# RMSNorm and SiLU on one core: the first three loads spread over both hardware DMA queues

## The chip, the cores and the metric

The kernel runs on one core of a Trainium2 chip. A core has engines that run side by side, each with its own instruction stream: VectorE (DVE in the profile), ScalarE (ACT), TensorE (PE), GpSimd (POOL) and SyncE (SP). Sixteen DMA engines move data between the chip's main memory (HBM) and the on-chip memory of 128 partitions (SBUF). Here ScalarE issues the loads and SyncE the stores, each over a hardware queue of its own; an issued transfer is cut into packets that the sixteen DMA engines carry.

The metric is the device time of one launch in microseconds (us), the median of several runs. Beside it there is one profiled execution, with every instruction and every DMA packet in its trace.

## The reference

```python
def setup_inputs():
    batch, seq_len, hidden = 8, 1024, 2048
    return {
        "x": np.random.randn(batch, seq_len, hidden).astype(np.float32),
        "gamma": np.random.randn(hidden).astype(np.float32),
        "eps": np.float32(1e-5),
    }

def reference(x, gamma, eps):
    rms = np.sqrt(np.mean(x ** 2, axis=-1, keepdims=True) + eps)
    out = gamma * x / rms
    return (out * (1 / (1 + np.exp(-out)))).astype(np.float32)
```

So 8192 rows of 2048 float32 are read, each row is divided by its root mean square, multiplied by gamma and passed through SiLU, and 8192 rows are written: 67.1 MB in and 67.1 MB out.

## The kernel before

The rows are cut into 16 blocks of 512 rows. A block lies in one tile `xt` of 128 partitions; a partition holds `J = 4` consecutive rows of x, 32 KB that are contiguous in main memory. Six tiles (`BUFS`) rotate, so a load needs the tile that the store six blocks before has left. All arithmetic on a block is done in place, and the store goes out from the same tile.

A block passes through these steps:

- `load` (line 54): one transfer of 4 MB, issued from ScalarE's queue.
- `squares_scalar` (line 65) and `squares_vector` (line 73): the sums of squares of its four rows per partition, one or two rows on ScalarE, the others on VectorE. The squares themselves go to a tile in PSUM that nobody reads.
- `root` on ScalarE (line 82) and `invert` on VectorE (line 87): the reciprocal of the root mean square.
- `multiply` on VectorE (line 92): row times reciprocal times gamma, one instruction per row.
- `silu` on ScalarE (line 98): two instructions, of two rows each, and then `store` (line 102), one transfer of 4 MB, issued from SyncE's queue.

The order of the work is written out by hand under `tc.manual_schedule()`. On each engine the instructions run in that order, and a DMA that an engine issues stands in the same order: an issue from ScalarE comes only after the ScalarE instructions ahead of it have been handed over. Semaphores between engines and DMAs are put in by the framework. It has eight for DMAs that it gives out in turn, so an issue can also carry a wait on an earlier transfer that had the same one.

At the start the six loads are issued one after another from ScalarE's queue. Then come two small fills on VectorE, a first activation on ScalarE that loads a table, and gamma's transfer of 8 KB, issued from SyncE (line 111). TensorE spreads gamma over all 128 partitions by multiplying it with a row of ones (line 114), and VectorE copies the result to `g` (line 115). The first use of `g` is `multiply(0)`.

The loop over blocks has three forms. For the first three blocks (`SOON`) the order is multiply(b), squares of b+1 on ScalarE, silu(b) with its store, squares of b+1 on VectorE, root(b+1). For the others up to block 13 the squares and the root of b+1 come first and multiply(b) and silu(b) after them. Block 14 goes in the first order again. Load b+3 is issued in the middle of `squares_scalar(b+1)`, behind its first activation, for blocks 6 to 15; since that activation needs block b+1, at most two loads are under way from then on. The last block is finished by a multiplication with gamma on VectorE and SiLU with the reciprocal as its scale on ScalarE (lines 152 and 154), and one last store.

Of the kernel before, what the change touches and what calls it, by code (L numbers as in the profile page):

```python
# [1 line left out]

# [4 lines left out]

ACT = mybir.ActivationFunctionType
ALU = mybir.AluOpType


@with_exitstack
def kernel(
    ctx: ExitStack,
    tc: tile.TileContext,
    x: bass.AP,
    gamma: bass.AP,
    eps: bass.AP,
    out: bass.AP,
):  # L20

    nc = tc.nc
    P = nc.NUM_PARTITIONS
    f32 = mybir.dt.float32
    x2 = x.flatten_outer_dims()
    o2 = out.flatten_outer_dims()  # L30
    n, d = x2.shape
    J = 4
    BUFS = 6
    nblk = n // (P * J)
    xb = x2.rearrange("(b p j) d -> b p (j d)", p=P, j=J)
    ob = o2.rearrange("(b p j) d -> b p (j d)", p=P, j=J)

    singles = ctx.enter_context(tc.tile_pool(name="singles", bufs=1))
    pool = ctx.enter_context(tc.tile_pool(name="pool", bufs=BUFS))
    small = ctx.enter_context(tc.tile_pool(name="small", bufs=2))  # L40
    psum = ctx.enter_context(tc.tile_pool(name="psum", bufs=1, space=bass.MemoryType.PSUM))

    Q = 4
    w = d // Q
    g = singles.tile([P, d], f32)
    eps_t = singles.tile([P, 1], f32)
    ones = singles.tile([P, P], f32)
    junk_a = psum.tile([P, d], f32, name="junk_a")
    junk_v = psum.tile([P, d], f32, name="junk_v")
    blocks, sss, rmss, rstds = {}, {}, {}, {}  # L50

    def load(b):
        xt = pool.tile([P, J * d], f32, name="xt")
        nc.scalar.dma_start(out=xt, in_=xb[b])  # L54
        blocks[b] = xt

    def row(b, j):
        return blocks[b][:, j * d:(j + 1) * d]

    def squares_scalar(b, loads=()):  # L60


        sss[b] = small.tile([P, J], f32, name="ss")
        for j in range(share(b)):
            nc.scalar.activation(out=junk_a, in_=row(b, j), func=ACT.Square,  # L65
                                 accum_out=sss[b][:, j:j + 1])
            if j == 0:
                for s in loads:
                    load(s)

    def squares_vector(b):
        for j in range(share(b), J):
            nc.vector.tensor_tensor_reduce(  # L73
                out=junk_v, in0=row(b, j), in1=row(b, j), scale=1.0, scalar=0.0,
                op0=ALU.mult, op1=ALU.add, accum_out=sss[b][:, j:j + 1])

    def share(b):
        return 1 if 4 <= b <= 12 and b % 2 == 0 else 2

    def root(b):  # L80
        rms = small.tile([P, J], f32, name="rms")
        nc.scalar.activation(out=rms, in_=sss.pop(b), func=ACT.Sqrt, scale=1.0 / d, bias=eps_t)  # L82
        rmss[b] = rms

    def invert(b):
        rstd = small.tile([P, J], f32, name="rstd")
        nc.vector.reciprocal(out=rstd, in_=rmss.pop(b))  # L87
        rstds[b] = rstd

    def multiply(b):  # L90
        for j in range(J):
            nc.vector.scalar_tensor_tensor(out=row(b, j), in0=row(b, j), scalar=rstds[b][:, j:j + 1],  # L92
                                           in1=g, op0=ALU.mult, op1=ALU.mult)

    def silu(b):
        for h in range(0, J, 2):
            cols = slice(h * d, (h + 2) * d)
            nc.scalar.activation(out=blocks[b][:, cols], in_=blocks[b][:, cols], func=ACT.Silu)  # L98
        store(b)

    def store(b):
        nc.sync.dma_start(out=ob[b], in_=blocks[b])

    with tc.manual_schedule():

        for b in range(BUFS):
            load(b)
        nc.vector.memset(ones, 1.0)  # L108
        nc.vector.memset(eps_t, float(eps))
        nc.scalar.activation(out=junk_a[:, 0:1], in_=ones[:, 0:1], func=ACT.Square)  # L110
        nc.sync.dma_start(out=g[0:1, :], in_=bass.AP(tensor=gamma.tensor, offset=gamma.offset, ap=[[d, 1], [1, d]]))
        for c in range(Q):
            cols = slice(c * w, (c + 1) * w)
            nc.tensor.matmul(junk_v[:, cols], ones[0:1, :], g[0:1, cols], start=True, stop=True)  # L114
        nc.vector.tensor_copy(out=g, in_=junk_v)  # L115

        last = nblk - 1
        SOON = 3  # L120
        squares_scalar(0)
        squares_vector(0)
        root(0)
        invert(0)
        for b in range(last):
            loads = [b + 3] if BUFS <= b + 3 < nblk else []
            if b < SOON:
                multiply(b)
                squares_scalar(b + 1, loads)
                silu(b)  # L130
                squares_vector(b + 1)
                root(b + 1)
            elif b < last - 1:
                squares_scalar(b + 1, loads)
                squares_vector(b + 1)
                root(b + 1)
                multiply(b)
                silu(b)
            else:
                multiply(b)  # L140
                squares_scalar(b + 1)
                silu(b)
                squares_vector(b + 1)
                root(b + 1)
            if b + 1 < last:
                invert(b + 1)


        for j in range(J):
            if j == J // 2:  # L150
                invert(last)
            nc.vector.tensor_mul(out=row(last, j), in0=row(last, j), in1=g)  # L152
        for j in range(J):
            nc.scalar.activation(out=row(last, j), in_=row(last, j), func=ACT.Silu,  # L154
                                 scale=rstds[last][:, j:j + 1])
        store(last)


# [1 line left out]
_INS = ['x', 'gamma', 'eps']  # L160
_OUTS = [((8, 1024, 2048), 'float32')]

_NUMBERS = {'eps': 9.999999747378752e-06}


# [26 lines left out]
```

## Time and profile before

| What | us |
| --- | --- |
| Median of 3 runs (317.01 to 317.69) | 317.03 |
| Span of the profiled execution, first to last instruction | 315.03 |
| VectorE busy, 157 instructions | 235.3 |
| ScalarE busy, 136 instructions | 213.8 |
| TensorE busy, 8 instructions | 7.2 |
| ScalarE idle for VectorE in front of silu (line 98) | 27.0 |
| VectorE idle for loads in front of its squares (line 73) | 42.3 |
| ScalarE idle for loads in front of its squares (line 65) | 22.5 |
| A load, issue to landing, shortest / median / longest | 12.3 / 38.7 / 81.8 |
| A store, issue to landing, shortest / median / longest | 13.5 / 28.6 / 33.7 |

The page of a profile gives the busy time of each engine, its share in 40 equal slices of the span, the DMA queues with their packets and bytes, and the chain of work that ended last. Further views give every instruction in order of time, who waited for whom, and busy time in stretches that one chooses.

Two queues carry nearly everything: 67.11 MB over the queue of ScalarE's issues (q10) and 67.12 MB over that of SyncE's issues (q1), at a mean of 426 GB/s over the span. These are some of the issues in order of time (start, duration, engine's queue and line, what):

```profile
0.73 2.97 ACTq L54 DMA_DIRECT2D xt<-in_x_dram  x6
0.73 0.34 SPq L111 DMA_DIRECT2D g<-in_gamma_dram  x1
...
66.81 0.33 ACTq L54 DMA_DIRECT2D xt<-in_x_dram  x1
...
84.99 0.34 ACTq L54 DMA_DIRECT2D xt<-in_x_dram  x1
```

The first six loads and gamma are issued at once, at 0.73; load 6 follows at 66.81 and load 7 at 84.99. The stores begin at 35.27.

### The profile page before, as it was taken

The page shows a single profiled execution, that of the slowest core. Times are in us where ns is not written, and L with a number is a line of the kernel's source. Part 1 is how long each engine was busy: PE and PEld are TensorE (multiplying, and loading weights), DVE is VectorE, ACT ScalarE, POOL GpSimd, SP SyncE. Part 2 cuts the span into 40 slices and gives each one's busy share as a digit, 9 for nine tenths or more (in the row PEclk, how much of TensorE's full clock was granted, in tenths as well). Part 3 has the DMA queues.
Part 4 walks back from the last instruction along what each step waited for, and adds up shares of the span by engine and source line. Part 5 has one row for each costly group of instructions (what it writes and reads, how often), then busy time and mean ns, then how long its engine had stood idle before and what let it go on. Part 6 is the DMA issues. An engine that isn't in the chain of part 4 may idle for free.

```text
span 315.0 us, 437 instructions
## 1 busy us (share of the span) xinstructions
PE 7.2 (2%) x8; PEld 2.5 (1%) x8; DVE 235.3 (75%) x157; ACT 213.8 (68%) x136; POOL 0.2 (0%) x4
## 2 busy tenths in 40 slices
PE   6200000000000000000000000000000000000000
PEld 3000000000000000000000000000000000000000
DVE  0679597979995795957959489593996939999600
ACT  1349998972799258782687727877288768779910
POOL 0000000000000000000000000000000000000000
DMA  8999999999999999999999999999999999999996
GB/s 334 399 466 399 399 466 399 466 399 466 399 467 404 459 416 449 420 445 420 445 420 445 420 445 420 445 424 445 420 445 429 437 429 437 429 437 433 433 433 300
DMA packets 4612, 134.24 MB, mean 426 GB/s; under 512 B 513, under 2 KB 513, under 8 KB 513
## 3 DMA queue, kind: packets, MB, share of 16 engines
q10 hardware_dynamic: 2304, 67.11, 49.8%
q1 hardware_dynamic: 2306, 67.12, 49.4%
q14 instruction: 2, 0.02, 0.0%
HBM read 67.12 MB, written 67.11 MB: 426 GB/s over the span
## 4 chain that ended last, share of the span: by engine, by line
DMA 68%; DVE 14%; ACT 11%; issue 2%; ACTq 1%; DVEq 0%
DMA xt<-in_x_dram 68%; DVE xt L92 9%; DVE junk_v L73 5%; ACT xt L98 4%; ACT junk_a L65 3%; ACT xt L154 2%; ACT L82 1%; ACTq L187 1%; ACT L154 0%; ACT L98 0%; ACT rms L82 0%; DVE ss L73 0%; DVE rstd L87 0%; ACTq L54 0%; ACTq L82 0%
## 5 line engine op out<-in xcount | busy, mean ns | idle before, releaser
L92 DVE SCALAR_TENSOR_TENSOR xt<-xt,rstd,g 128x2048 f32<-128x2048 f32 x60 | 137.0, 2345 | 0.1
L98 ACT ACTIVATE xt<-xt 128x4096 f32<-128x4096 f32 x30 | 108.3, 3615 | 27.0 <-DVE xt L92 27.0
L73 DVE CUSTOM_DVE_ANT_0 junk_v<-xt 128x2048 f32<-128x2048 f32 x37 | 85.1, 2299 | 43.0 <-DMA xt<-in_x_dram 42.3
L65 ACT ACTIVATE junk_a<-xt 128x2048 f32<-128x2048 f32 x27 | 50.6, 1876 | 22.8 <-DMA xt<-in_x_dram 22.5
L82 ACT ACT_TABLE_LOAD x15 | 19.2, 1283 | 27.4 <-DVE ss L73 27.3
L98 ACT ACT_TABLE_LOAD x14 | 18.0, 1283 | 0.2
L87 DVE RECIPROCAL rstd<-rms 128x4 f32<-128x4 f32 x16 | 2.7, 171 | 8.4 <-ACT rms L82 8.4
L152 DVE TENSOR_TENSOR xt<-xt,g 128x2048 f32<-128x2048 f32 x4 | 8.9, 2279 | 0.0
L115 DVE COPY g<-junk_v 128x2048 f32<-128x2048 f32 x1 | 2.3, 2292 | 8.6 <-PE junk_v L114 8.6
L82 ACT ACTIVATE rms<-ss,eps_t 128x4 f32<-128x4 f32 x16 | 4.8, 297 | 5.7 <-DVE ss L73 5.5
L154 ACT ACTIVATE xt<-xt,rstd 128x2048 f32<-128x2048 f32 x4 | 7.7, 1990 | 0.0
L114 PE MATMUL junk_v<-g,ones 1*128 1x512 f32 x8 | 7.2, 1073 | 2.4 <-DMA g<-in_gamma_dram 2.4
L73 DVE DVE_READ_ACCUMULATOR2_ANT ss<- 128x1 f32 x37 | 5.2, 140 | 0.0
L65 ACT ACTIVATION_READ_ACCUMULATOR junk_a<-xt 128x1 f32 x27 | 5.0, 186 | 0.0
L110 ACT ACT_TABLE_LOAD x1 | 1.3, 1283 | 3.7 <-issue 3.7
L114 PEld LDWEIGHTS junk_v<-g,ones 1*128 1x128 f32 x8 | 2.5, 326 | 5.5 <-issue 5.5
L154 ACT ACT_TABLE_LOAD x1 | 1.3, 1283 | 0.0
L108 DVE MEMSET ones<- 128x128 f32 x1 | 0.2, 165 | 0.8 <-PEq L173 0.8
L110 ACT ACTIVATE junk_a<-ones 128x1 f32<-128x1 f32 x1 | 0.2, 174 | 0.0
L173 POOL MEMSET const-bfloat16-1.0<- 128x1 bf16 x1 | 0.1, 103 | 0.0
L173 POOL MEMSET const-uint8-127<- 128x1 uint8 x1 | 0.1, 103 | 0.0
L173 POOL MEMSET const-float32-0.0<- 128x1 f32 x1 | 0.1, 99 | 0.2 <-issue 0.2
(2 smaller groups left out, 0.2 us busy)
## 6 DMA issues: line engine op xcount, KB each, us to landing
xt<-in_x_dram ACTq DMA_DIRECT2D x16, 4096.0 KB, 38.7
out_dram<-xt SPq DMA_DIRECT2D x16, 4096.0 KB, 28.6
g<-in_gamma_dram SPq DMA_DIRECT2D x1, 8.0 KB
```

The costliest lines, as they stand in the source:

```text
L65: nc.scalar.activation(out=junk_a, in_=row(b, j), func=ACT.Square, accum_out=sss[b][:, j:j + 1])
L73: nc.vector.tensor_tensor_reduce(out=junk_v, in0=row(b, j), in1=row(b, j), scale=1.0, scalar=0.0, op0=ALU.mult, op1=ALU.add, accum_out=sss ...
L82: nc.scalar.activation(out=rms, in_=sss.pop(b), func=ACT.Sqrt, scale=1.0 / d, bias=eps_t)
L87: nc.vector.reciprocal(out=rstd, in_=rmss.pop(b))
L92: nc.vector.scalar_tensor_tensor(out=row(b, j), in0=row(b, j), scalar=rstds[b][:, j:j + 1], in1=g, op0=ALU.mult, op1=ALU.mult)
L98: nc.scalar.activation(out=blocks[b][:, cols], in_=blocks[b][:, cols], func=ACT.Silu)
L110: nc.scalar.activation(out=junk_a[:, 0:1], in_=ones[:, 0:1], func=ACT.Square)
L114: nc.tensor.matmul(junk_v[:, cols], ones[0:1, :], g[0:1, cols], start=True, stop=True)
L115: nc.vector.tensor_copy(out=g, in_=junk_v)
L152: nc.vector.tensor_mul(out=row(last, j), in0=row(last, j), in1=g)
L154: nc.scalar.activation(out=row(last, j), in_=row(last, j), func=ACT.Silu, scale=rstds[last][:, j:j + 1])
L187: with _tile.TileContext(nc) as tc:
```

## The change

The loads of blocks 0 and 1 are each cut into two transfers: columns 0 to 4095 of the tile (the first two rows of a partition) over ScalarE's queue, columns 4096 to 8191 over SyncE's. Block 2 is loaded whole over SyncE's queue, where it stands in front of the stores. Blocks 3 and later are loaded over ScalarE's queue as before. Gamma's transfer is issued first, in front of the loads, still over SyncE's queue. No arithmetic is changed, and the order of the instructions on VectorE, TensorE and GpSimd stays as it was.

```diff
     BUFS = 6
+    PAIRED = 2
...
     def load(b):
         xt = pool.tile([P, J * d], f32, name="xt")
-        nc.scalar.dma_start(out=xt, in_=xb[b])
+        if b < PAIRED:
+            half = J * d // 2
+            nc.scalar.dma_start(out=xt[:, :half], in_=xb[b][:, :half])
+            nc.sync.dma_start(out=xt[:, half:], in_=xb[b][:, half:])
+        elif b == PAIRED:
+            nc.sync.dma_start(out=xt, in_=xb[b])
+        else:
+            nc.scalar.dma_start(out=xt, in_=xb[b])
         blocks[b] = xt
...
     with tc.manual_schedule():
 
+        nc.sync.dma_start(out=g[0:1, :], in_=bass.AP(tensor=gamma.tensor, offset=gamma.offset, ap=[[d, 1], [1, d]]))
         for b in range(BUFS):
             load(b)
         nc.vector.memset(ones, 1.0)
         nc.vector.memset(eps_t, float(eps))
         nc.scalar.activation(out=junk_a[:, 0:1], in_=ones[:, 0:1], func=ACT.Square)
-        nc.sync.dma_start(out=g[0:1, :], in_=bass.AP(tensor=gamma.tensor, offset=gamma.offset, ap=[[d, 1], [1, d]]))
```

On SyncE's queue the order is now gamma, the second half of block 0, the second half of block 1, block 2, and then the sixteen stores; on ScalarE's it is the first half of block 0, the first half of block 1, and blocks 3, 4 and 5. The framework's semaphores are given out in the new order, and with that the issue of block 5 from ScalarE carries a wait on gamma's transfer, which it did not before.

## The prediction

> **What bounds the kernel now.** I read the busy slices of the page first, then the queue table, then busy time and DMA by stretch, then the chain of waits, and last the trace's records of single DMA packets. In the slices:
>
> ```profile
> DVE  0679597979995795957959489593996939999600
> ACT  1349998972799258782687727877288768779910
> DMA  8999999999999999999999999999999999999996
> ...
> q10 hardware_dynamic: 2304, 67.11, 49.8%
> q1 hardware_dynamic: 2306, 67.12, 49.4%
> ```
>
> VectorE and ScalarE have holes everywhere; the DMA row has none between its first and its last slice. The two queues (q10 carries ScalarE's loads, q1 SyncE's gamma and stores) take 99.2% of sixteen engines' span. By stretch:
>
> ```profile
> 4.00:36.00 32.00, 5.57 (x7) 1.66 (x5) 20.95 (x14) 19.93 (x16) 0.00 (x0) 1.00 0.99 429
> 42.00:276.00 234.00, 0.00 (x0) 0.00 (x0) 188.89 (x127) 164.94 (x102) 0.00 (x0) 1.00 1.00 433
> 280.00:312.00 32.00, 0.00 (x0) 0.00 (x0) 16.25 (x11) 20.59 (x13) 0.00 (x0) 1.00 1.01 434
> ```
>
> The last column is GB/s. Loads alone (first row), loads and stores together (second) and stores alone (third) all run at the same rate. So the DMA engines have one ceiling, whoever asks, and the two queues share it; I call it the line.
>
> The packet records say how the span is made. Each block is 128 rows of 32 KB, so each of 16 DMA engines carries 8 packets per block and 256 in all for 16 loads and 16 stores. A 32 KB record takes 1.213 us, and records follow each other every 1.210 us (blocks 1 and 2 end 9.68 us apart, 9.68 / 8). The first packets start at 1.75 us on the first engine and 2.48 on the last; the last ends at 313.70. In between: 256 x 1.210 = 309.8; the first packet of an engine takes some 2.0 instead of 1.21 (ramp, 0.79); one load packet on every engine near 37.7 us, just before that engine's first store packet, takes some 1.81 (0.60, the "join" below); the stagger of starts is 0.73. Sum 311.9, against 313.70 - 1.75 = 311.95. There is no hole left to close. The join is visible in the stretches too:
>
> ```profile
> 36.00:40.00 4.00, 0.00 (x0) 0.00 (x0) 3.08 (x3) 3.96 (x5) 0.00 (x0) 1.00 1.07 393
> 40.00:277.80 237.80, 0.00 (x0) 0.00 (x0) 192.69 (x128) 168.04 (x104) 0.00 (x0) 1.00 1.00 432
> ```
>
> 393 GB/s where the first store comes in, 432 ever after. Span 315.03, of which 313.70 is reached by the last packet; the median of the runs, 317.03, lies 2.00 above the span, and I carry those 2.00 over.
>
> The chain of waits tells another story, which matters for a rival:
>
> ```profile
> 240.28 38.73 DMA xt<-in_x_dram
> 279.01 0.02 issue
> 279.03 2.01 ACT junk_a L65 x2
> ...
> 298.79 1.89 ACT xt L154
> ```
>
> It ends in the last block's arithmetic, after which the last store is issued at 300.71. But the previous store's packets hold the line until 302.80, when the last store's first packet starts; an issue comes to the line after some 1.1 us (store 0 issued at 35.27, its effect from 36.4; load 0 issued at 0.73, first packet at 1.75). So the last store arrives 302.80 - 300.71 - 1.1 = 1.0 us before it is needed, and the line, not the chain, sets the end.
>
> **The change part by part.**
>
> *Issues at the start.* SyncE gets three more issues behind gamma's (two halves, block 2), ScalarE's queue one fewer (5 for 6, of 2.97 us in all). SyncE has nothing else before 35.27; ScalarE's next real work waits for block 0 until 13.12, after 7.92 idle. Price 0. In the built program block 5's issue waits for gamma's transfer, and ScalarE's first table load is behind it; TensorE starts on gamma at 2.40, and the fifth issue would come near then anyway. Block 5 isn't carried before 60 us. Price 0, and 7.9 us of cover.
>
> *Halves of blocks 0 and 1.* Bytes and line are the same, so block 0 ends 9.7 us after the ramp and block 1 9.7 later, as now (ScalarE starts on them at 13.12 and 22.77). Each engine carries 32 packets of 16 KB in place of 16 of 32 KB. No 16 KB packet is in the trace. The nearest rows are its 8 KB packets: 307 ns the shortest, 329 for gamma's, against 303 for a quarter of 1.213 us, so 4 to 26 ns for a packet more: 16 x 0.004 = 0.06 to 16 x 0.026 = 0.42 us. I take 0.2, near the middle, since either row is one kind of 8 KB packet. Two more transfers mean four more completion records of 9 ns each on an engine at most: nothing.
>
> The Trainium skill ("DMA: Bandwidth & Descriptors", section "Anatomy of one DMA") gives a fixed cost of about 2.0 us for each DMA on GpSimd's path, which speaks against cutting transfers up; as an estimate from it, two more in series would make the sum 4 us longer, near 320.6. The trace has loads 0, 1 and 2 end to end on one queue with 9.68 us each and no gap, so that cost is covered wherever another packet waits.
>
> *Block 2 beside block 3.* Once blocks 0 and 1 are in (about 21.6), ScalarE's queue holds blocks 3, 4, 5 and SyncE's holds block 2. From 40 us on the records of the two queues alternate packet by packet, so blocks 2 and 3 both end near 21.6 + 16 x 1.21 = 41.0, against 32.0 and 44.7 now. What is late: ScalarE's squares of block 2 start at 41.4 and not 36.76; they take 4.04, the table load 1.29, silu of block 1 7.2, so store 1 is issued near 54.0 and not 49.92. VectorE isn't held: it reaches block 2 at 46.15. The root of block 2 follows silu of block 1 and is 3.1 later (55.7 for 52.58), and so are multiply(2), store 2 (68.7 for 65.63) and load 6, which sits behind root(3) on ScalarE's queue (near 70 for 66.81).
>
> Store 0, issued at 35.27 as now, stands behind block 2 on SyncE's queue and starts at 41.0. With block 4 it holds the line to 60.4. Store 1 comes at 54.0 + 1.1, 5.3 us early. With block 5 it holds the line to 79.8; store 2 is 10 us early, load 6 8.7 us. Store 3, 3.1 late at 91.4, is 6.6 us ahead of 99.1. Load 7, behind silu of block 3 at 87.6, is 10 ahead. Neither queue runs dry, so the 9 us of later landing cost 0; with the least cover, 5.3 us, gone, the loads would take the freed line until they run out too.
>
> By the skill's page on DMA, section "Queues, rings and completion order", an engine drains a packet of some 9 to 17 descriptors from one ring before it turns to the next; a ring holds 8 data packets per block here, so blocks would go by whole: block 2 in by about 31, block 3 by 41, or the other way round. The trace alternates single 32 KB records; by either, the line is full and the sum the same.
>
> *The end.* At 41.0 four loads are in and no store, where now some 0.4 block less of loads has gone when stores begin. Block 15 is then in at 60.4 + 11 x 19.36 = 273.4 (now 277.8). The last store is issued 300.71 - 279.01 = 21.7 after landing, near 295.5; the line wants it at 273.4 + 3 x 9.68 = 302.4. The cover grows from 1.0 to some 5.8 us. Worth 0, for the line still has all 32 blocks to carry.
>
> *The join.* Now SyncE's queue turns from empty (gamma long gone) to busy near 36.4 and every engine loses 0.60. After the change it turns busy near 2.2, in the ramp, when the engines stand waiting for their first data, and block 2 is in front of store 0, so it isn't empty when the stores begin. Bounds: -0.60 (hidden in the ramp and not paid again) and +0.60 (paid in the ramp and again at the first store). I take -0.60: the stretched row falls where a queue gets its first work, and that moment moves into 0.79 us in which the line waits anyway.
>
> *Sum.* 315.03 + 0.2 - 0.6 = 314.6; + 2.0 = **316.6 us**. With the bounds of both: 315.03 - 0.6 + 0.06 to 315.03 + 0.6 + 0.42, that is 316.5 to 318.05.
>
> **Rivals.**
>
> *The join stays* (0.27): it belongs to the first store, since that is the only place where the trace has it, and gamma's turn on the same queue shows none. Then 315.03 + 0.2 + 2.0 = 317.2. Against it: gamma is one packet on one engine, and shows little.
>
> *The tail shortens* (0.06): read by the chain of waits, the last block lands 4.4 us sooner and the end comes 4.4 sooner, 312.6. Against it: the line has no gap in which those 4.4 us could be saved.
>
> *Two load queues run slower than one* (0.15), the slower side. Place: the first 41 us, where each engine now carries 32 packets of 16 KB and 16 of 32 KB, switching between two loads at nearly each of these 48. If a switch exposes some latency, as the first packet does (0.79), it is paid on the line. From 0.026 a switch (gamma's excess): 48 x 0.026 = 1.25; with the join not hidden 315.03 + 1.25 + 2.0 = 318.3, hidden 317.7. It decides over no change by 0.2% from (0.63 + 0.6) / 48 = 0.026 if the join is hidden, from 0.013 if not. Against it: in the long middle load and store packets alternate with no gap at all; but no row has two loads alternating.
>
> **How the numbers follow.** Forecast 0.52, join stays 0.27, slower rival 0.15, tail 0.06. A measurement of this kernel can tell about 0.2%, 0.63 us, from no change, so "faster" is under 316.40 and "slower" over 317.66. The forecast, 0.2 above that bound with terms known to some 0.2, falls under it in about 3 of 10: 0.16, and with the tail about 0.21 faster. The slower rival lies beyond 317.66 at its price, and the join's upper bound for a little of the rest offsets where it is smaller: 0.15. Same 0.64. The range goes from 315.9, the forecast less 0.7 (the spread of the three runs, 317.69 - 317.01), to 318.0, past the join at both upper bounds less 0.05 and into the slower rival.
>
> **What would show it.** Right: blocks 2 and 3 landing together near 41.4; store 1 issued near 54; the last store near 295.5; the DMA rate at 429 to 434 in every stretch, and no dip to 393 where the first store begins. Wrong: a dip still there, near 41 (join stays); under 425 between 4 and 41 (slower rival); a DMA slice under 9 in the middle (a queue dry); a last packet much before 313 (tail).

## The result and the profile after

The changed kernel takes 317.14 us (median of 22 runs, 316.80 to 318.84), the kernel before, on the same chips, 316.84 (22 runs, 316.69 to 317.69). The ratio is 1.0016, 95% interval 1.0009 to 1.0023: slower by some 0.5 us by the ratio and by 0.30 by the medians. The mean moves more than the middle, because the runs spread. Of the changed kernel's 22 runs nine lie over 317.4, of the other's one; the thirteen below have a median of 317.0, against 316.83 for the 21 of the kernel before.

The profiled execution has a span of 316.4 us and belongs to a run of 318.19, so it shows the spread and not the middle. The busy slices and queues of its page:

```profile
DVE  0379795297999999969698496975959669999000
ACT  0659609998169968993887538964488768699500
POOL 0000000000000000000000000000000000000000
DMA  7999999999999999999999999999999999999995
...
q1 hardware_dynamic: 2738, 75.51, 55.3%
q10 hardware_dynamic: 2160, 58.72, 43.4%
```

8.39 MB (two halves and block 2) went from q10, ScalarE's queue, to q1, SyncE's. The DMA row is as full as before between its first and its last slice: the line, the rate that both queues share, has no hole there in either kernel. Busy time by stretch (the last column is GB/s):

```profile
4.00:36.00 32.00, 5.63 (x7) 1.66 (x5) 20.96 (x14) 19.46 (x16) 0.00 (x0) 1.00 1.01 435
...
44.00:48.00 4.00, 0.00 (x0) 0.00 (x0) 4.00 (x3) 1.03 (x1) 0.00 (x0) 1.00 0.87 320
48.00:274.00 226.00, 0.00 (x0) 0.00 (x0) 184.92 (x125) 169.67 (x106) 0.00 (x0) 1.00 1.00 433
280.00:312.00 32.00, 0.00 (x0) 0.00 (x0) 12.73 (x9) 17.11 (x9) 0.00 (x0) 1.00 1.01 437
313.00:315.10 2.10, 0.00 (x0) 0.00 (x0) 0.00 (x0) 0.00 (x0) 0.00 (x0) 1.00 0.04 16
```

435 GB/s in the first row: two load queues at once are as fast as one. The dip is still there, and moved from 36 to 40 us to 44 to 48, where the first store now begins. The last row is new: for the last 2 us almost nothing moves. The packet records say why. Sorted into 16 DMA engines by following each record to the one that starts where it ends, 15 engines end between 312.96 and 313.78 us, as before (312.95 to 313.70), and one at 315.09. That engine lost 0.47 us at 79.5 and 80.8, where load 6 begins on it, and then 0.06 to 0.37 at 101.8, 121.5, 138.6, 141.1, 160.7, 218.0 and 238.7, mostly in steps of some 19.4 us, the time in which one load and one store pass; from 55 us on it lost 2.0 us in all. A packet of 8 KB for the engines' instructions (queue 14, at 89.14) cut into another engine: it took 0.31 us, the packet behind it was stretched by 0.36, and after that this engine lost only 0.09 and ended at 313.78. A second such packet, at 102.39, fell on a third engine, which ended at 313.52. The rest lost nothing of the kind.

The timeline of the changed kernel, cut to what moved (start, duration, engine and line, what; in brackets the idle time before it and what ended it):

```profile
1.14 0.83 SPq L58 DMA_DIRECT2D xt<-in_x_dram  x2
1.63 9.15 ACTq L62 DMA_DIRECT2D xt<-in_x_dram  x3
...
10.80 1.28 ACT L119 ACT_TABLE_LOAD   x1 [10.80 <-DMA xt<-in_x_dram]
...
46.97 1.88 ACT L73 ACTIVATE junk_a<-xt 128x2048 f32<-128x2048 f32 x1 [9.38 <-DMA xt<-in_x_dram]
...
59.46 0.34 SPq L110 DMA_DIRECT2D out_dram<-xt  x1
...
74.11 0.33 SPq L110 DMA_DIRECT2D out_dram<-xt  x1
...
75.29 0.34 ACTq L62 DMA_DIRECT2D xt<-in_x_dram  x1
...
297.19 0.33 SPq L110 DMA_DIRECT2D out_dram<-xt  x1
```

Block 2 is used from 46.97 (before: 36.76), store 1 is issued at 59.46, store 2 at 74.11, load 6 at 75.29 (before: 66.81). By then block 5 had left the line (last packet ends at 74.83), so ScalarE's queue sent nothing until load 6's first packet at 79.36, and stores had the line alone. From there on a load's last packet ends shortly before a store's, over and over. On fifteen engines it is 4.84 us before, the time of four packets; on the late engine it is some 2.45 us, two packets. The difference arises at load 6: on the fifteen its first packet (79.36 to 79.68) goes ahead of the last packet of store 1, on the late engine (80.80) behind it. In the kernel before, a load's last packet ends 12.1 us before one store's and 7.3 after the one ahead (122.5; 115.2 and 134.6).

### The profile page after: what moved, and what is told of

Same layout as the page of the kernel before. It is cut to its first block, busy times and chain, and to the rows that moved or that the text cites. A ratio compares the mean times of both kernels' runs of the same rounds, so it can differ in the third digit from the quotient of the medians.

```text
span 316.4 us, 442 instructions
## 1 busy us (share of the span) xinstructions
PE 7.2 (2%) x8; PEld 2.5 (1%) x8; DVE 235.1 (74%) x157; ACT 213.3 (67%) x136; POOL 0.2 (0%) x4
## 4 chain that ended last, share of the span: by engine, by line
DMA 50%; DVE 22%; ACT 15%; issue 5%; ACTq 1%; SPq 0%; DVEq 0%
DMA xt<-in_x_dram 37%; DMA out_dram<-xt 13%; DVE xt L100 13%; DVE junk_v L81 9%; ACT xt L106 7%; ACT junk_a L73 3%; ACT xt L162 2%; ACT L90 1%; ACT L106 1%; ACTq L195 1%; ACT L162 0%; ACT rms L90 0%; DVE ss L81 0%; SPq L58 0%; DVE rstd L95 0%
```

## The experiments

Each run is compared with the kernel before on the same chip. "Gap" below is the time from the last packet of a load to that of the next store, near 120 us, over all engines together where no engine is named. "Stretch" is what packets took beyond 1.213 us (32 KB) or 0.611 us (16 KB) between 55 and 285 us, summed and divided by 16 engines, so that the first stores are left out.

**The changed kernel again.** No edit.

> The changed kernel once more, to see whether its spread comes back. In its profiled run 15 of 16 DMA engines ended between 312.96 and 313.78 us, as in the kernel before (312.95 to 313.70), and one engine at 315.09, after some ten packets that took longer than 1.25 us. Theory A (one engine now and then loses time because loads and stores run in another phase to each other than before): runs spread from 316.9 to over 318 again, median some 0.3 above the kernel before. Theory B (the halves, or two load queues at once, cause it): the same here. Theory C (chance of the runs so far): within 0.2 of the kernel before, all runs within 0.5.

317.02 (12 runs) against 316.94: 1.0020, 1.0007 to 1.0033. Seven runs lie between 316.85 and 317.03, five between 318.19 and 318.52. The spread is the kernel's own, so theory C is out. The profiled execution is one of the low runs (span 315.1): the gap is 4.8 on every engine, and the one that lost 0.67 us near 89.2 to the instruction packet loses nothing afterwards.

**Gamma first, alone.** `load` as in the kernel before.

> Gamma's issue moved to the front alone; all loads over ScalarE's queue as before. All theories: no change, within 0.1 us of the kernel before, and no spread; one packet on every engine stretched to some 1.8 us where the first store begins.

316.85 against 316.94 (1.0001, 0.9992 to 1.0009), all but one run up to 317.02 and one at 317.73. Nothing.

**Halves alone.**

```diff
-        elif b == PAIRED:
-            nc.sync.dma_start(out=xt, in_=xb[b])
```

> Blocks 0 and 1 in halves over two queues; block 2 stays on ScalarE's queue. 16 KB packets followed each other every 0.607 us in the changed kernel's trace, so 16 pairs cost 16 x (1.214 - 1.210) = 0.07 us. Theory A: the loads' lead over the stores is nearly that of the kernel before, so +0.1 and no spread. Theory B: +0.3 or more, with runs up to 318. The queue of the stores has then been busy once and is empty again when the first store comes: the stretch of some 0.6 us should be there at the first store in either.

317.03 against 316.94 (1.0001, 0.9992 to 1.0009), highest 317.58. Gap 12.1. Packets of 16 KB off two load queues followed each other every 0.607 us. Theory B falls, and with it the slower rival of the prediction. Load packets were stretched at the first store, as in the kernel before.

**Block 2 alone.**

```diff
-        if b < PAIRED:
-            half = J * d // 2
-            nc.scalar.dma_start(out=xt[:, :half], in_=xb[b][:, :half])
-            nc.sync.dma_start(out=xt[:, half:], in_=xb[b][:, half:])
-        elif b == PAIRED:
+        if b == PAIRED:
```

> Block 2 alone moved to SyncE's queue in front of the stores (gamma first); blocks 0 and 1 whole over ScalarE's. Loads and stores then run in another phase than before. Theory A: spread up to 318 and a median 0.2 to 0.4 above the kernel before. Theory B: within 0.1 and no spread. The stretch of 0.6 us: if it belongs to a queue that turns from empty to busy it comes where block 2 joins, near 5 us, and not at the first store; if it belongs to the first store it comes there, some 40 us in.

321.70 (4 runs, 321.47 to 322.31) against 316.94: 1.0153, 1.0140 to 1.0166. More than ten times what I expected, and the clue. Block 2 now shares the line with block 0, which is used from 20.32 and not 13.12, so store 0 is issued at 44.90; load 6, at 76.44, again comes after its queue has run dry (73.6). Gap 3.4. On nearly every engine one or two packets in every 19.6 us are stretched, 3.12 us an engine in all. The line is never empty, yet slower (busy time and GB/s by stretch):

```profile
48.00:274.00 226.00, 0.00 (x0) 0.00 (x0) 190.06 (x128) 166.17 (x106) 0.00 (x0) 1.00 1.00 425
```

425 GB/s with a DMA share of 1.00. In the records the stretch sits where one queue passes from a transfer to its next and the other does so two packets later, most often on the first or second load packet behind that place. That made the phase theory: what costs is the end of a load shortly before the end of a store on the same DMA engine. As loads and stores share the line one to one, the gap that the start sets stays for the rest. To test it I moved the gap in the kernel before, without touching a load.

**Store 0 late by two, four, three and one squares.**

```diff
+                if b == 0:
+                    for i in range(2):
+                        nc.scalar.activation(out=junk_a, in_=row(1, 0), func=ACT.Square)
                 silu(b)
```

> The kernel before, with two more ScalarE squares of 1.9 us (results unused) in front of the first silu, so that store 0 comes some 3.8 us later; loads untouched. Phase theory: what costs is the end of a load and the end of a store falling within some 2 to 4 us of each other on a DMA engine (2 to 3.4 us in the run with block 2 alone over SyncE's queue, where all engines had one stretched packet in every 19.5 us; 7.3 us in the kernel before, where none had). Loads run 3.8 us longer alone and store 0 ends 3.8 us later, so the ends move together by 7.6: from 7.3 apart to nearly none. Expected 319 to 322 us, with stretched packets every 19.4 us on many engines. Rival (the loss comes from SyncE's queue carrying loads, or block 2 landing late): 316.9, since the line stays full.

Three of the five runs took 318.57, 320.21 and 320.33, the other two 329.52 and 333.03; the three against 316.88: 1.0081, 1.0058 to 1.0103. The loss is there without any load on SyncE's queue. The only profile is of the longest run, with a gap of 2.4; its DMA row has slices at 6 tenths near the end, which the gap alone doesn't explain, so its rate and its stretch aren't those of the three. The rate in the middle:

```profile
48.00:274.00 226.00, 0.00 (x0) 0.00 (x0) 172.42 (x117) 152.11 (x94) 0.00 (x0) 1.00 1.00 422
```

> The same with four such squares, so store 0 comes some 7.6 us later and the ends move by some 15: past each other to some 8 us on the other side. Phase theory: back to 316.9 within 0.3, no recurring stretched packets, though more is delayed than in the run with two. Theory that lateness itself costs: at least as slow as with two.

316.97 (10 runs, 316.68 to 317.46) against 316.88: 1.0001, 0.9992 to 1.0010. Gap 7.3. Twice the delay, and the loss is gone:

```profile
48.00:274.00 226.00, 0.00 (x0) 0.00 (x0) 195.14 (x130) 168.52 (x106) 0.00 (x0) 1.00 1.00 434
```

So lateness itself costs nothing.

> The kernel before with three extra squares, between the runs with two (320.3) and four (317.0): ends move by some 11.4, from 7.3 on one side to some 4 on the other, as in the changed kernel. Phase theory: near the edge, 316.9 to 318.5, some runs or single engines with recurring stretched packets.

317.08 (10 runs, 316.73 to 317.78) against 317.06: 1.0003, 0.9994 to 1.0012. The gap came out at 5.9 and not 4, and it is clean. By engine it is 4.84 on fifteen and 7.3 on one.

> The kernel before with one extra square: ends move by 3.8, from 7.3 to some 3.5 on the same side. Phase theory, if both sides cost alike: 317 to 318.5 with recurring stretched packets on some engines; if only the order load end, then store end costs: 316.9, clean.

319.35 (5 runs, 317.26 to 319.60) against 317.06: 1.0060, 1.0038 to 1.0082. The gap began at 0.8 (load 61.9, store 62.7), with stretched packets on several engines between 50 and 97 us; then the last of the store's packets passed ahead of the last of the load's (store 101.4, load 102.4), and from 105 to 285 us a single packet is stretched by more than 0.1. Sorted by engine, six have the load's end one packet (1.2 us) ahead of the store's there, the others the store's end one or two packets ahead. So neither of these does harm; the 2.3 us that its last engine lost fall between 55 and 100 us. I had expected a gap of 3.5; the estimate was off by 2.7.

**Three blocks in halves.**

```diff
-    PAIRED = 2
+    PAIRED = 3
...
-        elif b == PAIRED:
-            nc.sync.dma_start(out=xt, in_=xb[b])
```

> The changed kernel, but block 2 in halves too, so that it lands near 32 us again and store 0 follows on an empty queue near 39. Phase theory: the ends lie 7 us apart as in the kernel before; 24 pairs of 16 KB packets cost 24 x 0.0045 = 0.11 us: 316.9 to 317.1, no run over 317.8. Theory that load halves over two queues cause the spread: runs to 318 and over, as in the changed kernel.

317.12 (11 runs, 316.92 to 317.79) against 316.88: 1.0010, 1.0001 to 1.0018. Gap 12.1, stretch 0.05. 6.3 MB of loads over SyncE's queue (8.4 in the changed kernel), and a highest run of 317.79; what is left, some 0.2 to 0.3, is more than the 0.11 expected for the smaller packets.

**The changed kernel with its load 6 in time.**

```diff
                 squares_scalar(b + 1, loads)
-                silu(b)
-                squares_vector(b + 1)
-                root(b + 1)
+                if b == 1:
+                    squares_vector(b + 1)
+                    root(b + 1)
+                    silu(b)
+                else:
+                    silu(b)
+                    squares_vector(b + 1)
+                    root(b + 1)
```

> The changed kernel with one move: for block 1 the VectorE squares and the root of block 2 come before silu of block 1, so multiply(2) starts some 8 us sooner and load 6, which in the changed kernel's trace was issued at 75.29 when block 5 had left the line at 74.8, is issued near 67 to 68, ahead of that. Phase theory: ScalarE's queue never runs dry, loads and stores keep some 8 to 10 us between their ends (3.5 to 4.8 in the changed kernel), one engine no longer loses packet time every 19.4 us: median 316.9 to 317.1, no run over 317.8. Theory that the spread comes from loads on SyncE's queue or 16 KB packets: spread to 318.5 as before.

317.25 (11 runs, 317.03 to 317.39) against 317.06: 1.0005, 0.9996 to 1.0014. The spread is gone and no difference can be measured. From its timeline:

```profile
67.26 0.33 ACTq L62 DMA_DIRECT2D xt<-in_x_dram  x1
```

Load 6 is issued 9.0 us before block 5 leaves the line (76.3), the queue doesn't run dry, the gap is 9.2 and the stretch 0.06. Halves, block 2 over SyncE's queue and a late first store are all still in it.

**A small store first.** 64 KB of ones, into the place that the last store fills anew; in the second run behind gamma.

```diff
+        nc.sync.dma_start(out=ob[nblk - 1][:, :P], in_=ones)
```

> The kernel before, with a store of 64 KB (the ones, into the place that the last store fills anew) as the first thing on SyncE's queue. If the stretch of 0.6 us on every engine belongs to the first store of all, it moves to the first 5 us, where it may hide in the ramp, and is gone near 37: 316.3. If it belongs to stores joining a running stream of loads, it stays near 37: 316.9 plus up to 0.2 for 64 KB more. (With SyncE's queue already busy with loads since 5 us it still came at the first store in the changed kernel, so it isn't the queue turning busy.)

318.54 (6 runs, 317.58 to 319.93) against 316.88: 1.0054, 1.0036 to 1.0072. Gamma stood behind it, landed near 15 us and made store 0 ten us later (45.85), so the run isn't clean. Near 49 every engine has the stretched packet all the same.

> The early store of 64 KB again, now behind gamma, which in the first such run landed at 15 us and held up everything behind it. If that delay, and the phase it brought, made its loss, this run is at 316.9 to 317.2; the stretch of 0.6 us stays near 37, as it did (at 48) in the first. If the early store itself costs, it stays near 318.

317.31 (10 runs, 317.16 to 318.09) against 317.06: 1.0010, 1.0001 to 1.0019, about the 0.2 of its bytes. The stretch near 37 is there. So it doesn't belong to the first write of all but to the first block's store joining a stream of loads; I found no way to hide it. Why j1 lost more than j2, with a gap of 6.1 in its profiled execution, stays open; that execution is the shortest of the six. In it one engine has a gap of 2.4 us and loses nothing, so such a gap doesn't cost in every case.

Put in order, gap against stretch in the profiled executions (j1 and j2 are the two runs with the small store):

| Run | Gap, us | Stretch, us per engine | Median less that of before |
| --- | --- | --- | --- |
| one square | 0.8, later -1.0 | 0.36, nearly all before 105 us | +2.29 |
| two squares (its longest run) | 2.4 | 5.25 | +3.33, of three runs |
| block 2 alone | 3.4 | 3.12 | +4.76 |
| changed kernel (a high run) | 3.5; by engine 4.84, on the late one 2.45 | 0.20, mostly on the late engine | +0.30 |
| changed kernel again (a low run) | 4.8 | 0.07 | +0.08 |
| three squares | 5.9 | 0.06 | +0.02 |
| j1 (its shortest run) | 6.1 | 0.17 | +1.66 |
| four squares | 7.3 | 0.05 | +0.09 |
| changed, load 6 in time | 9.2 | 0.06 | +0.19 |
| before; gamma first; halves alone; three halves | 12.1 | 0.07; 0.07; 0.07; 0.05 | 0; -0.09; +0.09; +0.24 |
| j2 | 13.7 | 0.04 | +0.25 |

## Why the prediction was wrong

The forecast was 316.6, 0.4 under the time before; the kernel came out 0.30 slower. Both lie within the bound of 0.2% for no change, but the sign is the other one.

**What bounds it: right.** The line sets the end in both kernels. Two load queues carry 435 GB/s where one carries 429, a packet of 16 KB takes its half (0.607 against 1.210 / 2), and the tail by the chain of waits is worth nothing: the last store was issued at 297.19 against 300.71, and the end did not come sooner.

**The join: the step that failed first.** The sentence was "I take -0.60: the stretched row falls where a queue gets its first work, and that moment moves into 0.79 us in which the line waits anyway." SyncE's queue did get its first load work early, at 5.4 us, with no packet of its own or the other queue's stretched there beyond the ramp, and it was not empty when store 0 began. The load packets near 46.3 took 1.55 to 1.88 us all the same, a loss of 0.57 us an engine against 0.64 before. The rival "the join stays", at 317.2, was the right one; it was in the text with the right reason, that the trace has the stretch only at the first store. With the join left as it was and the halves at their measured 0.06 (below), the sum is 315.03 + 0.06 + 2.0 = 317.1, near where the low runs lie (317.0).

**"Neither queue runs dry": wrong.** Block 2 was to be used from 41.4 and was used from 46.97. A queue that gets work while the other is busy waits: the first half over SyncE's queue, issued at 1.14, had its first packet at 5.4, some 4 us later, with ScalarE's queue at work (store 0 in the kernel before: issued 35.27, first packet 39.45). I had put 1.1 us for this, from a queue with no rival and from the stretched load packets at 36.4, which were not yet the store. And the halves on SyncE's queue then alternated packet by packet with block 3's, 16 KB for 32 KB, until 25.9. Store 1 followed at 59.46 for 54.0, load 6 at 75.29 for 70, while blocks 3, 4 and 5, which had got ahead, left the line sooner, block 5 at 74.8 for 79.8. So the cover of 8.7 us was used up, and for 4.5 us more ScalarE's queue sent nothing; the stores took the freed line, as said, and nothing was lost there.

**What was missing: the gap.** Nothing in the sum had a price for where a load ends relative to a store. The runs above give it: free from 4.8 us up (j1 apart, whose loss stays open), and 4.8 us a kernel with block 2 alone, where it is two packets on most engines. The empty queue at 75 moved the gap from 12.1 to 4.84, two packets from what costs. In the high run, one DMA engine took up load 6 one turn later than the others, had a gap of 2.45 and lost a little more with most blocks; in the low run all sixteen have 4.8 and lose nothing. The move that issues load 6 in time takes the spread away, so it is shown that the empty queue makes the spread; the step from the late turn to the late end rests on one high run and one low one. The instruction packet isn't its start: in the high run it fell on another engine, and in both runs the engine that it hit lost next to nothing afterwards. Why one engine takes load 6 later in some runs stays open.

**Smaller points.** 16 KB packets: +0.2 was taken; 16 x (2 x 0.607 - 1.210) is 0.06, and halves alone measured +0.09 within an interval that holds no change. The wait that block 5's issue carries is on the first half of block 0, not on gamma, as I read it and as the text on the change says: the three issues at line 62 last until 10.78, just after that half landed (10.42), and the table load behind them starts at 10.80. It cost nothing, as ScalarE starts on block 0 at 12.30, but the cover was thinner than the 7.9 us that I named. In the kernel before, the first packet of the last store starts at 303.27 and not at 302.80, so the cover in front of it was 1.5 us and not 1.0; nothing in the sum hung on it.

## What to carry to other kernels

With the DMA engines full from end to end, the change of queues won nothing of the time that it seemed to free; in such a kernel ask also where it leaves transfers relative to each other, for that relation is kept as long as loads and stores share the line evenly. A bimodal or spread set of runs with a full DMA row is a reason to look at single engines: here one of sixteen ended 1.3 us late, and the page showed it only in the last slice. When work is moved to a second queue while the first is busy, take the delay from a place where both are at work (here some 4 us from issue to first packet), not from an idle line (1.0).

## What the runs showed of the hardware

Not expected were three things. Where a queue passes from one 4 MB transfer to the next, it leaves out a turn, and two packets of the other queue run back to back (in the kernel before on all sixteen engines between 110 and 150 us). When a load ends two packets (2.4 us) before a store on the same DMA engine, the two missed turns lie side by side, and there packets are mostly stretched: by 3.12 us an engine with block 2 alone, or 0.26 for each of the twelve pairs of blocks, and by 2.0 us on the late engine of the changed kernel. One packet (1.2 us) either way, a store two packets ahead, or a gap from 4.8 us up cost nothing once the runs had settled; what in a DMA engine does this the runs don't tell. The first 4 MB store into a stream of loads costs an engine once, 0.57 us in the mean of the sixteen in the changed kernel and up to 0.98 with gamma first; this comes even when the store's queue is already at work or a smaller store has gone before. And the profiled executions of both kernels each have two 8 KB packets for the engines' instructions (at 93.94 and 108.51 us in the kernel before), each of which holds up one DMA engine by 0.42 to 0.67 us.
